# Moving transposes, filter loads and shared-expert products in a Hyena–SSD–MoE block, and removing the edge products of its long convolutions

## The chip, the cores and the metric

The kernel runs on one core of a Trainium2 chip. The metric is the device time of one execution in microseconds (us), the median of several runs. A core has five engines, each with its own instruction queue that runs strictly in order: TensorE (PE, matrix products), VectorE (DVE), ScalarE (ACT), GpSimd (POOL) and SyncE (SP, which only issues transfers here). Sixteen DMA engines move the data. POOL and ACT can issue transfers as well.

## The reference

One encoder block for 1024 tokens of width 1024, in float32:

```python
proj = u @ w_in + b_in                      # 1024 x 11328
k_spec = hyena_filters(seq, ...)            # implicit filters -> spectra
y_hy = hyena_mixer(p_hy, ..., k_spec, hy_bias) @ w_hy_branch
y_ssd = ssd_mixer(p_z, p_xbc, p_dt, ...) @ w_ssd_branch
g_hy, g_ssd = split(sigmoid(p_gate), 2)
mix = (g_hy * y_hy + g_ssd * y_ssd) @ w_out + b_out
h = layer_norm(alpha * h + mix)
h = layer_norm(alpha * h + moe(h))          # 64 experts, top 8, and a shared expert

def fft_long_conv(u, k_spec, bias):         # twice per channel
    uf = rfft(u, n=2 * seq)
    y = irfft(uf * k_spec, n=2 * seq)[:seq]
    return y + u * bias
```

The SSD mixer is a scan over 8 groups of 4 heads, in 8 chunks of 128 tokens and in both directions; its output is normalised by the root of a mean square for each group.

## The kernel before, in words

All wide products are made of three products of rounded parts (high by high, low by high, high by low), 128x512 each. Four stages follow one another.

**Front (to about 1325 us).** The input projection runs in slots. One slot is one block of 128 columns of `w_in`: eight k-steps of three products for two token halves (L174; in the trace a pair of halves is one entry x2, so a k-step has three entries). Everything else of this stage is hooked into slots by a table: `at(slot, when, f)` calls `f` at the beginning of a slot, ahead of k-step 0 to 7, or at its end. That table fixes the order on every queue. For each scan group g, `start[g]` is its first slot b. Its jobs are:

- `t1`, `t1x`, `t2`: transposes on PE of B and X into banks S, O and Y of PSUM (L291), each copied out by ACT (L292); `t2` ends with seven weighings of X on POOL (L313).
- `load_bc`, `side_e`: SP loads decay rows (`bcs`), DVE adds a mask (L379), ACT takes eight exponentials (L383).
- `states`, `states1`: PE products for the states (L329), a chain on DVE that adds them up (L331, L333, L334).
- `post1`: normalisation of the group that ends (DVE, short steps), then eight scalings on ACT (L431).
- `post2`: transposes of the result on PE (L438), copied out by ACT with a scale (L439), and stored by SP (L440).

The end of one group (`post1` and `post2` at slots b + 11 and b + 12) falls into the first slots of the next. Groups 1, 3 and 5 (`FILL4`) have one slot fewer, so that both `post2` fall into one slot. Between slots DVE and ACT run the short convolution of the block before (`conv`: L180, L183; `silu`: L592, L594), and POOL or DVE makes the low part of the weights (L163).

**Filters (1310 to 1530 us).** `hy_prep` loads `hS` and `w4` from POOL's queue. `hy_filters` loads decay tables `dec` (three buffers) and `brow` from SP's queue and the cosine tables from POOL's; PE makes filter blocks (L926, L927, and L929 for the bias row), DVE multiplies them by `dec` (L932), ACT and POOL or DVE split them (L73, L74), and PE multiplies by the cosines.

**Convolutions (1530 to 1770 us).** Eight items (four channel blocks, two filter orders). An item is folded (`fold`, L807 to L810), transposed (`analyse`, copied to `sdf` by ACT), multiplied by four frequency blocks kt (`forward`, L1054), combined with the filter spectrum on DVE (L1070 to L1090), and transformed back (L1107 to L1110). The even and odd samples lie in rows ty of `sdf`. One unpaired sample has a table of its own, `Fe`, and one extra matmul for each kt (L1056).

**Output projection and experts (1770 us to the end).** In `merge` the router's scores are 64-column products (`scores`, L78 to L80 into bank D). The shared expert is a generator, cut into chunks of three 128x512 products, that `route`, `early` and the end of the function advance. Then come 64 experts: SP loads weights `eraw`, ACT and DVE split them (`ehi` L1627, `elo` L1633), POOL gathers tokens (L1640), PE multiplies (L78 to L80).

Of the kernel before, what the change touches and what calls it, by code (L numbers as in the profile page):

```python
# [19 lines left out]
P = 128  # L20
# [4 lines left out]
KT = D // P  # L25
ALPHA = 2.0 ** 0.25


# [13 lines left out]
class Kern:  # L42
# [231 lines left out]
    def ssd_jobs(self, pool, pool2, g, tl):  # L274
# [149 lines left out]
        def post1():  # L424
            ss = S["ss"]
            TS(ss, ss, 1.0 / 256, 4e-5, ALU.mult, ALU.add)
            S["rs"] = pool.tile([P, 8], F32, name="rs", bufs=2)
            self.rsqrt(S["rs"], ss, pool, 8)
            for c in range(8):
                yz = S["zs"][:, c, :]  # L430
                nc.scalar.activation(yz, yz, AF.Copy, scale=S["rs"][:, c:c + 1])  # L431

        def post2(q):
            yo = S["zs"][:, :, q * P:(q + 1) * P]
            for h in range(2):
                pt = self.bank("SY"[h])
                for j in range(4):
# [4 lines left out]
        return dict(load_bc=load_bc, states1=states1, t1x=t1x, t1=t1, t2=t2, states=states, zs_tr=zs_tr, pe1=pe1, pe3=pe3, side_e=side_e, side_a=side_a, side_b=side_b,  # L442
                    side_c=side_c, post1=post1, post2=post2)

# [19 lines left out]
    def front(self):  # L464
# [4 lines left out]
        with ExitStack() as c2:  # L469
# [147 lines left out]
            for g in range(8):  # L617
                j = jobs[g]
                b = start[g]
                at(b, 4, j["t1"])  # L620
                at(b, 6, j["t1x"])
                at(b + 1, 3, j["t2"])
                at(b + 1, "end", j["states"])
                at(b + 2, 1, j["states1"])
                for q in range(2):
                    at(b + 2 + q, 3, lambda j=j, q=q: j["zs_tr"](q))
                at(b, "end", lambda j=j: j["load_bc"](0))
                for c in range(8):
                    at(b + 1 + c, "first", lambda j=j, c=c: j["side_e"](c))
                    at(b + 2 + c, 4, lambda j=j, c=c: j["pe1"](c))  # L630
                    at(b + 2 + c, "side", lambda j=j, c=c: j["side_b"](c))
                for c in range(8):
                    at(b + 1 + c, "side", lambda j=j, c=c: j["side_a"](c))
                    at(b + 3 + c, 5, lambda j=j, c=c: j["pe3"](c))
                    at(b + 4 + c, "begin", lambda j=j, c=c: j["side_c"](c))
                at(b + 11, "begin", j["post1"])
                for q in range(2):
                    def f(j=j, q=q, sl=b + 11 + q):
                        j["post2"](q)()
                    if q and g in FILL4:  # L640
                        at(b + 11, "side", f)
                    else:
                        at(b + 11 + q, 7 - 6 * q, f)
# [161 lines left out]
    def fold(self, u, sd):  # L805
        nc = self.nc
        rev = free(u[:, 512:513], [[-1, 512]])  # L807
        nc.vector.tensor_tensor(sd[:, 0], u[:, 512:1024], rev, ALU.add)
        nc.gpsimd.tensor_tensor(sd[:, 1], rev, u[:, 512:1024], ALU.subtract)
        nc.gpsimd.tensor_copy(sd[:, 1, 0:1], u[:, 0:1])  # L810

# [3 lines left out]
    def hy_prep(self):  # L815
# [14 lines left out]
        def s_load(m):  # L830
            nc.gpsimd.dma_start(S[m], self.S_d[:, m])
            load(m, slice(0, 256))
        s_load(0)
        nc.sync.dma_start(self.brow[0], a["hy_bias"][:, :, 0:256])
        yield
# [5 lines left out]
    def hyena(self):  # L841
        nc, a, tc = self.nc, self.a, self.tc
        self.K_d = self.scratch("K", (2, 4, 4, P, 1024))
        self.yhy_d = self.scratch("yhy", (D, L))
        if True:
            self.fp = tc.alloc_tile_pool(name="hyf", bufs=1, reuse_waits="tile")
            self.fs = tc.alloc_tile_pool(name="hys", bufs=1, reuse_waits="tile")
            self.sds, self.folds, self.Kt = {}, {}, {}
            self.sgn = self.fs.tile([P, 1], F32, name="sgn")
            nc.sync.dma_start(self.sgn, a["c_sgn"])  # L850
            for _ in self.flt:
                pass
            self.hy_convs()
# [19 lines left out]
    def analyse(self, k, j, tag):  # L873
        nc = self.nc
        if j == 0:
            self.sds[k] = (self.fs if k % 2 == 0 else self.fa).tile([P, 4, 2, 256], F32, name=f"sdf{k % 2}")
        sd = self.folds.pop((k, j))
        for q in range(2):
# [9 lines left out]
            if q == 0:  # L888
                nc.scalar.copy(d, ps)
            else:  # L890
                nc.scalar.copy(d[:, 0], ps[:, 0])
                nc.scalar.activation(d[:, 1], ps[:, 1], AF.Copy, scale=self.sgn)

    def hy_filters(self):
# [10 lines left out]
        def load_dec(i):  # L905
            if i < len(steps):
                b, m = steps[i]
                for h in range(2):
                    decs[i, h] = kp.tile([P, 4, 256], F32, name="dec", bufs=3)
                    nc.sync.dma_start(decs[i, h], a["c_dec"][m, b, :, h * 4:(h + 1) * 4])  # L910
                if m == 0:
                    br[b] = self.brow[b % 2]
                    if b > 0:
                        nc.sync.dma_start(br[b], a["hy_bias"][:, :, b * 256:(b + 1) * 256])
# [43 lines left out]
        with ExitStack() as cx:  # L958
# [3 lines left out]
            for i, (b, m) in enumerate(steps):  # L962
                if i == 2:
                    nc.sync.dma_start(Fm, a["c_F"])
                    Fe = self.Fe = self.fp.tile([P, 512], F32, name="Fe")
                    nc.gpsimd.memset(Fe, 0.0)
                    nc.scalar.copy(Fe[0:1], Fm[0:1, 2, 0])
                    self.sd_load(0)
# [38 lines left out]
    def hy_convs(self):  # L1007
# [7 lines left out]
        with ExitStack() as cx:  # L1015
# [5 lines left out]
            gts, zs, Z, inv, fw, sto = {}, {}, {}, {}, {}, []  # L1021
            Fm, Fe, sgn = self.Fm, self.Fe, self.sgn

# [16 lines left out]
            def forward(k, kt):  # L1040
# [6 lines left out]
                for par in range(2):  # L1047
                    for q in range(2):
                        ty = 2 * q + par
                        out = ps[:, par, q * 256:(q + 1) * 256]  # L1050
                        edge = par == 0 and q == 0
                        fy, fs = (ty, ksl) if ty < 3 else (1, slice((kt + 2) % 4 * P, ((kt + 2) % 4 + 1) * P))
                        for mt in range(2):
                            mm(out, Fm[:, fy, mt, fs], sd[:, ty, mt], start=mt == 0, stop=mt == 1 and not edge)  # L1054
                        if edge:
                            mm(out, Fe[:, ksl], sd[:, 2, 0], start=False, stop=True)  # L1056
                yc = pool.tile([P, 512], F32, name="yc", bufs=1)
# [171 lines left out]
    def merge(self):  # L1229
# [107 lines left out]
        with ExitStack() as cx:  # L1337
# [113 lines left out]

            def scores(t):
                for k, (xh, xl) in enumerate(lhs(t)):
                    self.mm3(psl[:, t * 64:(t + 1) * 64], xh, xl, rt[0][:, k], rt[1][:, k], k == 0, k == 7)

# [92 lines left out]
            for t in range(4, 8):  # L1548
# [4 lines left out]
                if t == 4:  # L1553
                    for _ in sh_down(0, hb):
                        pass
                    hb = sh_h(sg1)
                scores(t)
            wp.release()
            self.tabs()
            fill = rest(hb)  # L1560

# [758 lines left out]
def consts():  # L2320
# [23 lines left out]
    c["c_dec"] = np.ascontiguousarray(dec.transpose(0, 3, 2, 1, 4))  # L2344
    f = 4 * np.arange(512) + 1

# [11 lines left out]
    F[0][0] = 0.5  # L2358
    F[2][0] = w[0]
    c["c_F"] = np.ascontiguousarray(np.concatenate(F).astype(np.float32).reshape(3, 2, P, 512).transpose(2, 0, 1, 3))  # L2360
# [47 lines left out]
```

## Time and profile before

| | |
|---|---|
| median of 3 runs | 3216.88 us (3214.09 to 3218.8) |
| the profiled execution | 3221.08 us, its span 3219.3 us |
| PE, DVE, ACT, POOL busy | 94%, 69%, 48%, 28% |
| mean granted TensorE clock | 0.971 |

The span runs from the first to the last instruction. In the rows below a timeline entry is start, duration, engine, line, operation, tile written and tiles read; square brackets hold the idle time of the engine ahead of it and what ended that. A granted clock of 1.00 is 2.4 GHz and 0.50 is 1.2 GHz.

### The profile page before, as it was taken

What the parts mean: (1) busy time and instruction counts of PE and PEld (TensorE: products, weight loads), DVE (VectorE), ACT (ScalarE), POOL (GpSimd) and SP (SyncE); (2) the same over time, 40 slices, a digit from 0 to 9 for tenths busy, and PEclk for the clock granted to TensorE, in tenths of its full rate; (3) what the DMA queues carried; (4) which work ended last, traced back from release to release, by engine and by line L of the source; (5) the groups of instructions that cost most, each with busy time, mean ns of one, the idle gap of its engine ahead of it and who ended that gap; (6) DMA issues with size and microseconds to landing.
All of it is one profiled execution on the core that took longest, in us unless ns stands there. A gap on an engine that the chain in (4) does not pass through costs nothing.

```text
span 3219.3 us, 41385 instructions
## 1 busy us (share of the span) xinstructions
PE 3034.7 (94%) x14955; PEld 2457.2 (76%) x14955; DVE 2226.7 (69%) x3146; ACT 1544.8 (48%) x2573; POOL 901.6 (28%) x670
## 2 busy tenths in 40 slices
PE   8898999899989989899999999999899999999991
PEld 6786878787878878688888888887677777777771
DVE  6665666566666757565998244466688888888875
ACT  3544464546445544322222321242577777777772
POOL 2202020202011211343020041021254555555643
PEclk9999999999999999899999999998899999999996
DMA  4333432323242333654324444533899999999996
GB/s 140 74 88 75 99 86 82 92 86 82 81 102 71 109 82 98 173 184 173 125 92 144 138 163 132 161 105 128 261 322 324 327 331 323 316 312 317 321 300 173
DMA packets 343899, 546.54 MB, mean 170 GB/s; under 512 B 24617, under 2 KB 242509, under 8 KB 334989
## 3 DMA queue, kind: packets, MB, share of 16 engines
q1 hardware_dynamic: 316781, 450.54, 44.0%
q0 software_dynamic: 25760, 89.14, 11.3%
q10 hardware_dynamic: 1152, 4.19, 0.3%
q8 instruction: 119, 1.95, 0.2%
q14 instruction: 87, 0.71, 0.1%
HBM read 434.48 MB, written 109.32 MB: 169 GB/s over the span
## 4 chain that ended last, share of the span: by engine, by line
PE 79%; DVE 7%; ACT 5%; DMA 4%; issue 4%; POOL 1%; SPq 0%; ACTq 0%; DVEq 0%; POOLq 0%
PE bankA L174 24%; PE bankA L1312 8%; PE bankA L78 8%; PE bankA L79 7%; PE bankA L80 7%; PE bankI L1110 3%; PE bankA L1054 3%; PE bankA L1897 2%; PE bankB L1655 2%; PE bankA L1899 2%; PE bankY L373 2%; ACT bcs L383 1%; DMA bcs<-scr_at 1%; DMA scr_ace<-yo,sidx 1%; PE bankD L2116 1%
## 5 line engine op out<-in xcount | busy, mean ns | idle before, releaser
L174 PE MATMUL bankA<-xth,whi 128*128 128x512 f32 (+1 forms) x1424 | 474.3, 414 | 1.1 <-ACT whi L158 0.9
L174 PE MATMUL bankA<-xth,wlo 128*128 128x512 f32 (+1 forms) x1424 | 445.5, 394 | 1.5 <-POOL wlo L163 1.5
L174 PE MATMUL bankA<-xtl,whi 128*128 128x512 f32 (+1 forms) x1424 | 446.7, 395 | 0.0
L1633 DVE TENSOR_TENSOR elo<-eraw,ehi 128x2048 fp32r<-128x2048 f32 (+1 forms) x198 | 438.4, 2217 | 8.6 <-DMA scr_acc<-sr 8.6
L1627 ACT CAST ehi<-eraw 128x2048 fp32r<-128x2048 f32 (+1 forms) x198 | 356.8, 1858 | 5.8 <-DVE sr L1493 3.4
L174 PEld LDWEIGHTS bankA<-xth,wlo 128*128 128x128 f32 (+1 forms) x1424 | 268.7, 189 | 63.5 <-POOL wlo L163 1.9
L174 PEld LDWEIGHTS bankA<-xtl,whi 128*128 128x128 f32 (+1 forms) x1424 | 269.5, 189 | 60.7 <-DVE xtl L74 0.4
L174 PEld LDWEIGHTS bankA<-xth,whi 128*128 128x128 f32 (+1 forms) x1424 | 260.7, 191 | 54.8 <-issue 5.6
L1640 POOL DMA_INDIRECT xg<-scr_h,gidx x96 | 225.5, 2349 | 167.3 <-PE bankB L1655 128.2
L163 POOL TENSOR_TENSOR wlo<-wraw,whi 128x1024 fp32r<-128x1024 f32 (+1 forms) x35 | 83.4, 2383 | 638.8 <-ACT whi L158 623.3
L558 ACT ACTIVATE pin<-bankA,par 128x512 f32<-128x512 f32 x112 | 71.1, 687 | 331.6 <-PE bankA L174 331.4
L79 PE MATMUL bankA<-elo,xgh 128*128 128x512 f32 (+1 forms) x512 | 204.1, 399 | 9.0 <-DVE elo L1633 9.0
L78 PE MATMUL bankA<-ehi,xgh 128*128 128x512 f32 (+1 forms) x512 | 208.9, 408 | 0.3 <-ACT ehi L1627 0.3
L80 PE MATMUL bankA<-ehi,xgl 128*128 128x512 f32 (+1 forms) x512 | 203.2, 397 | 0.0
L383 ACT ACTIVATE bcs<-bcs,Acs 128x128 f32<-128x128 f32 x512 | 157.1, 396 | 50.3 <-DVE bcs L379 50.2
L1676 POOL DMA_INDIRECT scr_ace<-yo,sidx x48 | 124.5, 2593 | 177.8 <-ACT yo L1675 86.2
L183 DVE SCALAR_TENSOR_TENSOR accxs<-pin,parh,accxs 128x1024 f32<-128x1024 f32 x64 | 103.2, 1613 | 64.2 <-ACT accxs L180 61.4
L1676 POOL DMA_INDIRECT scr_acc<-yo,sidx x48 | 100.3, 2090 | 132.1 <-DVE yo L1936 65.5
L313 POOL TENSOR_TENSOR xw<-Xtok,wst 128x256 f32<-128x256 f32 x112 | 114.3, 1046 | 79.8 <-ACT Xtok L292 67.4
L1054 PE MATMUL bankA<-sdf,Fm 128*128 128x256 f32 x512 | 122.2, 382 | 2.2 <-DVE U L1071 2.2
L379 DVE TENSOR_TENSOR bcs<-bcs,negm 128x1024 f32<-128x1024 f32 x64 | 78.1, 1220 | 63.7 <-DMA bcs<-scr_at 63.7
L79 PEld LDWEIGHTS bankA<-elo,xgh 128*128 128x128 f32 (+1 forms) x512 | 95.4, 186 | 33.5 <-DVE elo L1633 12.2
(555 smaller groups left out, 6948.2 us busy)
## 6 DMA issues: line engine op xcount, KB each, us to landing
eraw<-in_exp_w_gate_dram SPq DMA_DIRECT2D x128, 512.0 KB
eraw<-in_exp_w_up_dram SPq DMA_DIRECT2D x128, 512.0 KB
eraw<-in_exp_w_down_dram SPq DMA_DIRECT2D x64, 1024.0 KB
wraw<-in_w_in_dram SPq DMA_DIRECT2D x88, 512.0 KB
bcs<-scr_at SPq DMA_DIRECT2D x128, 256.0 KB
scr_K<-kout SPq DMA_DIRECT2D x32, 512.0 KB
Kt<-scr_K SPq DMA_DIRECT2D x32, 512.0 KB
scr_gate<-accf SPq DMA_DIRECT2D x16, 512.0 KB
```

The source lines that it names most:

```text
L78: mm(out, sh, mh, start=first, stop=False)
L79: mm(out, sh, ml, start=False, stop=False)
L80: mm(out, sl, mh, start=False, stop=last)
L174: mm(ps[h], wt[:, k, :n], x[:, h * 512:(h + 1) * 512], start=(k == 0 and f == 1), stop=(k == KT - 1 and l == 1))
L313: GT(hq(xw), hq(S["X"][:, c, :]), hb(self.wst, c, d, 64), ALU.mult)
L383: nc.scalar.activation(E[:, d, h], E[:, d, h], AF.Exp, bias=self.A[:, c, j:j + 1])
L1054: mm(out, Fm[:, fy, mt, fs], sd[:, ty, mt], start=mt == 0, stop=mt == 1 and not edge)
L1312: mm(ps[h], w[:, k], al[h][q], start=(k == 0 and st == 1), stop=(k == 7 and en == 1))
L1627: nc.scalar.copy(whl[p][0][:, c], wraw[p][:, c])
L1633: nc.vector.tensor_tensor(lo[:, c], wraw[p][:, c], hi[:, c].bitcast(F32), ALU.subtract)
L1640: nc.gpsimd.indirect_dma_start(out=t[:n, :], out_offset=None, in_=self.h_d, in_offset=bass.IndirectOffsetOnAxis(ap=tabs[r][s][0], axis=0))
L1676: nc.gpsimd.indirect_dma_start(out=self.acc_d if b % 2 else self.ace_d, out_offset=bass.IndirectOffsetOnAxis(ap=tabs[r][s][1], axis=0), in ...
```

## The change

**Front.** `t1`, `t1x` and `t2` stood at k-step 4, k-step 6 and k-step 3 of the next slot for all groups. Now they stand at 7, 7 and (next slot) 3 for group 0, at k-steps 2, 3 and 4 of the first slot for groups 1, 3, 5 and 7, and where they were for groups 2, 4 and 6. The eight scalings of `post1` become `post1s`; for groups 0, 2, 4 and 6 they move from the beginning of slot b + 11 to its k-step 5.

**Filters.** The first `brow` and the first two `dec` loads go to POOL's queue.

**Convolutions.** The 512 frequencies are renumbered, even ones first in each half. With that order the unpaired sample has one constant factor with alternating sign by kt, so it can be merged into the row of the middle sample: `fold` scales it, `analyse` keeps a second version `sde` of row 0 for odd kt, and the 32 extra matmuls, `Fe`, its memset and its copy go. Added are 16 ACT copies (128x128), 16 POOL subtractions (1x128) and 16 DVE operations (128x1); 16 POOL copies (128x1) become multiplications.

**Experts.** The generator of the shared expert starts ahead of `scores(4)`, and `scores` of token blocks 4 to 7 takes one chunk at each odd k, 16 in all.

```diff
+        def post1s():
             for c in range(8):
                 yz = S["zs"][:, c, :]
                 nc.scalar.activation(yz, yz, AF.Copy, scale=S["rs"][:, c:c + 1])
...
-                at(b, 4, j["t1"])
-                at(b, 6, j["t1x"])
-                at(b + 1, 3, j["t2"])
+                h = (7, 7, 11) if g == 0 else (4, 6, 11) if g - 1 in FILL4 else (2, 3, 4)
+                for n, w in zip(("t1", "t1x", "t2"), h):
+                    at(b + w // 8, w % 8, j[n])
...
                 at(b + 11, "begin", j["post1"])
+                at(b + 11, "begin" if g in FILL4 or g == 7 else 5, j["post1s"])
...
-        nc.gpsimd.tensor_copy(sd[:, 1, 0:1], u[:, 0:1])
+        nc.gpsimd.tensor_scalar(sd[:, 1, 0:1], u[:, 0:1], 2 * R2, None, ALU.mult)
+        nc.vector.scalar_tensor_tensor(sd[:, 0, 0:1], u[:, 0:1], R2, sd[:, 0, 0:1], ALU.mult, ALU.add)
...
+        nc.gpsimd.dma_start(self.brow[0], a["hy_bias"][:, :, 0:256])
         s_load(0)
-        nc.sync.dma_start(self.brow[0], a["hy_bias"][:, :, 0:256])
...
             if q == 0:
                 nc.scalar.copy(d, ps)
+                nc.scalar.copy(self.sde[k][:, j * P:(j + 1) * P], ps[:, 0, 0])
             else:
                 nc.scalar.copy(d[:, 0], ps[:, 0])
+                r0, e0 = self.sds[k][0:1, :, 0, j * P:(j + 1) * P], self.sde[k][0:1, j * P:(j + 1) * P]
+                nc.gpsimd.tensor_tensor(e0, r0[:, 0], r0[:, 2], ALU.subtract)
...
-                    nc.sync.dma_start(decs[i, h], a["c_dec"][m, b, :, h * 4:(h + 1) * 4])
+                    (nc.sync if i else nc.gpsimd).dma_start(decs[i, h], a["c_dec"][m, b, :, h * 4:(h + 1) * 4])
...
-                        edge = par == 0 and q == 0
+                        rows = [sd[:, ty, mt] for mt in range(2)]
+                        if ty == 0 and kt % 2:
+                            rows[0] = self.sde[k]
...
-                            mm(out, Fm[:, fy, mt, fs], sd[:, ty, mt], start=mt == 0, stop=mt == 1 and not edge)
-                        if edge:
-                            mm(out, Fe[:, ksl], sd[:, 2, 0], start=False, stop=True)
+                            mm(out, Fm[:, fy, mt, fs], rows[mt], start=mt == 0, stop=mt == 1)
...
-            def scores(t):
+            def scores(t, fill=None):
                 for k, (xh, xl) in enumerate(lhs(t)):
+                    if fill and k % 2:
+                        next(fill, None)
                     self.mm3(psl[:, t * 64:(t + 1) * 64], xh, xl, rt[0][:, k], rt[1][:, k], k == 0, k == 7)
...
-                    hb = sh_h(sg1)
-                scores(t)
+                    fill = rest(sh_h(sg1))
+                scores(t, fill)
             wp.release()
             self.tabs()
-            fill = rest(hb)
...
-    f = 4 * np.arange(512) + 1
+    f = 4 * np.concatenate([np.arange(o, o + 256, 2) for o in (0, 1, 256, 257)]) + 1
...
-    F[2][0] = w[0]
+    F[2][0] = np.sign(w[0]) / 4
```

ACT's queue where group 1 begins, before (`Btok` and `Xtok` are the copies behind `t1`, `t1x` and `t2`, `zs` the result of group 0):

```order
L431 ACTIVATE zs<-zs,rs 128x256 x8
L292 COPY Btok<-bankS 128x512
L292 COPY Btok<-bankO 128x512
L292 COPY Xtok<-bankS 128x4x128
L439 ACTIVATE zs<-bankS,par 128x4x128
L439 ACTIVATE zs<-bankY,par 128x4x128
L558 ACTIVATE pin<-bankA,par 128x512 x2
L158 ACTIVATE whi<-wraw 128x1024
L180 ACTIVATE accC<-pin,parh 128x1024
L383 ACTIVATE bcs<-bcs,Acs 128x128 x8
L439 ACTIVATE zs<-bankS,par 128x4x128
L439 ACTIVATE zs<-bankY,par 128x4x128
```

The same place of ACT's queue in the changed kernel, whose line numbers are larger by up to 3:

```order
L293 COPY Btok<-bankS 128x512
L293 COPY Btok<-bankO 128x512
L293 COPY Xtok<-bankS 128x4x128
L293 COPY Xtok<-bankO 128x4x128
L293 COPY Xtok<-bankS 128x4x128
L293 COPY Xtok<-bankY 128x4x128
L434 ACTIVATE zs<-zs,rs 128x256 x8
L442 ACTIVATE zs<-bankS,par 128x4x128
L442 ACTIVATE zs<-bankY,par 128x4x128
L561 ACTIVATE pin<-bankA,par 128x512 x2
L159 ACTIVATE whi<-wraw 128x1024
L181 ACTIVATE accC<-pin,parh 128x1024
```

The six copies now stand together ahead of the eight scalings; three of them stood behind the exponentials (L383) and the last two L439.

POOL's queue where the filters begin, before (`w4l`, `w4h` and `hS` are the filter network's operands):

```order
L831 DMA hS_10082<-scr_S 128x1024
L828 DMA w4h_10079<-scr_w4h 64x2x256 x2
L828 DMA w4l_10080<-scr_w4l 64x2x256
L948 DMA cose<-in_c_cose_dram 128x1024 x2
L831 DMA hS_10078<-scr_S 128x1024
L828 DMA w4h_10075<-scr_w4h 64x2x256 x2
L828 DMA w4l_10076<-scr_w4l 64x2x256
L951 DMA coso<-in_c_coso_dram 128x2048 x2
L74 TENSOR_TENSOR kl<-kr,kh 128x512
```

The same place of POOL's queue in the changed kernel:

```order
L838 DMA brow_10081<-in_hy_bias_dram 1x2x256
L836 DMA hS_10090<-scr_S 128x1024
L833 DMA w4h_10087<-scr_w4h 64x2x256 x2
L833 DMA w4l_10088<-scr_w4l 64x2x256
L920 DMA dec<-in_c_dec_dram 128x1024 x2
L958 DMA cose<-in_c_cose_dram 128x1024 x2
L836 DMA hS_10086<-scr_S 128x1024
L833 DMA w4h_10083<-scr_w4h 64x2x256 x2
L833 DMA w4l_10084<-scr_w4l 64x2x256
L961 DMA coso<-in_c_coso_dram 128x2048 x2
L75 TENSOR_TENSOR kl<-kr,kh 128x512
```

The two `dec` loads stand ahead of the cosine tables, the second set of `hS` and `w4`, and POOL's first split.

PE's queue at the scores of token block 6, in the changed kernel (`rth`, `rtl` are the router's weights in bank D; `wh`, `wl` and `ld` belong to the shared expert):

```order
L1452 MATMUL bankB<-ident,sr 128x128 x8
L79 MATMUL bankD<-rth,bh 128x64
L80 MATMUL bankD<-rtl,bh 128x64
L81 MATMUL bankD<-rth,bl 128x64
L79 MATMUL bankA<-wh,ld 128x512
L80 MATMUL bankA<-wl,ld 128x512
L81 MATMUL bankA<-wh,ld 128x512
L79 MATMUL bankD<-rth,bh 128x64
L80 MATMUL bankD<-rtl,bh 128x64
L81 MATMUL bankD<-rth,bl 128x64
L79 MATMUL bankD<-rth,bh 128x64
L80 MATMUL bankD<-rtl,bh 128x64
```

Before, the 24 products of a token block into bank D stood there without the 128x512 products between them; those stood behind the last product of `early`.

## Rows read from the trace of the kernel before

**Rows 1.** Busy time of each engine over the span, from the page

```profile
PE 3034.7 (94%) x14955; PEld 2457.2 (76%) x14955; DVE 2226.7 (69%) x3146; ACT 1544.8 (48%) x2573; POOL 901.6 (28%) x670
```

**Rows 2.** Stretches: PE, PEld, DVE, ACT, POOL busy (instructions), granted clock, DMA share, GB/s

```profile
1540.00:1760.00 220.00, 220.00 (x1072) 195.06 (x1072) 209.49 (x270) 51.00 (x139) 28.08 (x20) 1.00 0.34 109
...
2165.00:2190.00 25.00, 24.26 (x123) 22.83 (x123) 7.24 (x11) 5.59 (x9) 4.72 (x2) 0.60 0.18 70
...
2250.00:2260.00 10.00, 10.00 (x53) 8.34 (x50) 4.72 (x19) 0.77 (x2) 2.97 (x3) 1.00 0.50 171
...
2270.00:2280.00 10.00, 2.78 (x7) 2.20 (x8) 4.73 (x8) 4.49 (x5) 0.00 (x0) 0.50 0.70 239
```

**Rows 3.** Timeline of PE where group 1 begins

```profile
276.86 1.12 PE L291 MATMUL bankS<-ident,accxs 128*128 128x128 f32 x4 [9.09 <-ACT zs L439]
...
280.33 1.05 PE L174 MATMUL bankA<-xth,wlo 128*128 128x512 f32 x2
...
285.09 0.63 PE L174 MATMUL bankA<-xtl,whi 128*128 128x512 f32 x2
```

**Rows 4.** Timeline of ACT at the same place

```profile
254.18 3.32 ACT L431 ACTIVATE zs<-zs,rs 128x256 f32<-128x256 f32 x8 [3.09 <-DVE rs L462]
...
273.77 2.46 ACT L383 ACTIVATE bcs<-bcs,Acs 128x128 f32<-128x128 f32 x8 [8.24 <-DVE bcs L379]
276.13 0.67 ACT L439 ACTIVATE zs<-bankS,par 128x512 f32<-128x512 f32 x1
```

**Rows 5.** Timeline of DVE at the same place, and last where group 7 begins

```profile
272.51 1.23 DVE L379 TENSOR_TENSOR bcs<-bcs,negm 128x1024 f32<-128x1024 f32 x1 [16.09 <-DMA bcs<-scr_at]
273.66 5.31 DVE L183 SCALAR_TENSOR_TENSOR accC<-pin,parh,accC 128x1024 f32<-128x1024 f32 x4
...
280.44 1.67 DVE L594 SCALAR_TENSOR_TENSOR accC<-pin,accC 128x1024 f32<-128x1024 f32 x1 [0.46 <-ACT pin L592]
288.05 0.42 DVE L331 COPY st<-bankO 128x256 f32<-128x256 f32 x1 [5.94 <-PE bankO L329]
...
1211.03 0.42 DVE L331 COPY st<-bankO 128x256 f32<-128x256 f32 x1 [4.58 <-PE bankO L329]
```

**Rows 6.** Timeline of PE in the first slot of group 0

```profile
100.09 1.09 PE L291 MATMUL bankS<-ident,accB 128*128 128x128 f32 x4 [7.75 <-DVE accB L594]
```

**Rows 7.** The chain that ended last where the filters begin

```profile
1323.40 8.11 DMA scr_gate<-accf
1331.58 10.83 DMA dec<-in_c_dec_dram
```

**Rows 8.** Timelines of ACT, DVE and PE at the same place

```profile
1329.18 3.31 ACT L431 ACTIVATE zs<-zs,rs 128x256 f32<-128x256 f32 x8 [3.10 <-DVE rs L462]
1335.02 1.23 ACT L73 ACTIVATE kh<-kr 128x512 fp32r<-128x512 f32 x2 [2.54 <-DVE kr L932]
...
1342.53 1.29 DVE L932 TENSOR_TENSOR kr<-bankA,dec 128x512 f32<-128x512 f32 x2 [1.75 <-DMA dec<-in_c_dec_dram]
...
1348.27 1.12 PE L438 MATMUL bankS<-ident,zs 128*128 128x128 f32 x4 [7.81 <-ACT zs L439]
```

**Rows 9.** The extra products of line L1056: shortest, median, longest in ns; first, last start

```profile
L1056 PE MATMUL bankA<-sdf,Fe x64: 379/379/634, 1515.9 to 1743.4; 128*128 128x256 f32 x64
```

**Rows 10.** Timeline of DVE inside the convolutions

```profile
1616.70 0.15 DVE L1146 COPY zc<-y 128x1 f32<-128x1 f32 x1
...
1619.41 2.29 DVE L1077 TENSOR_TENSOR M<-U,Kt 128x1024 f32<-128x1024 f32 x1
...
1629.68 1.22 DVE L1077 TENSOR_TENSOR M<-U,Kt 128x1024 f32<-128x1024 f32 x1
```

**Rows 11.** Timeline of POOL at the same place

```profile
1618.26 2.36 POOL L1150 TENSOR_TENSOR zc<-zc,gt 128x1024 f32<-128x1024 f32 x1 [25.73 <-DVE zc L1149]
```

**Rows 12.** Timelines of SP and PE where the experts begin

```profile
2264.77 0.34 SPq L1616 DMA_DIRECT2D eraw<-in_exp_w_gate_dram  x1
...
2277.22 0.80 PE L79 MATMUL bankA<-elo,xgh 128*128 128x512 f32 x1 [9.02 <-DVE elo L1633]
```

More of the change, by code (lines that the diff above doesn't have):

```diff
@@ L26 @@
 ALPHA = 2.0 ** 0.25
+R2 = 2.0 ** 0.5
 def bcast(ap, dims):
@@ L442, in ssd_jobs @@
         return dict(load_bc=load_bc, states1=states1, t1x=t1x, t1=t1, t2=t2, states=states, zs_tr=zs_tr, pe1=pe1, pe3=pe3, side_e=side_e, side_a=side_a, side_b=side_b,
-                    side_c=side_c, post1=post1, post2=post2)
+                    side_c=side_c, post1=post1, post1s=post1s, post2=post2)
     def rsqrt(self, out, v, pool, n):
@@ L847, in hyena @@
             self.fs = tc.alloc_tile_pool(name="hys", bufs=1, reuse_waits="tile")
-            self.sds, self.folds, self.Kt = {}, {}, {}
+            self.sds, self.sde, self.folds, self.Kt = {}, {}, {}, {}
             self.sgn = self.fs.tile([P, 1], F32, name="sgn")
@@ L875, in analyse @@
         if j == 0:
-            self.sds[k] = (self.fs if k % 2 == 0 else self.fa).tile([P, 4, 2, 256], F32, name=f"sdf{k % 2}")
+            fp = self.fs if k % 2 == 0 else self.fa
+            self.sds[k] = fp.tile([P, 4, 2, 256], F32, name=f"sdf{k % 2}")
+            self.sde[k] = fp.tile([P, 256], F32, name=f"sde{k % 2}")
         sd = self.folds.pop((k, j))
@@ L964, in hy_filters @@
                     nc.sync.dma_start(Fm, a["c_F"])
-                    Fe = self.Fe = self.fp.tile([P, 512], F32, name="Fe")
-                    nc.gpsimd.memset(Fe, 0.0)
-                    nc.scalar.copy(Fe[0:1], Fm[0:1, 2, 0])
                     self.sd_load(0)
@@ L1021, in hy_convs @@
             gts, zs, Z, inv, fw, sto = {}, {}, {}, {}, {}, []
-            Fm, Fe, sgn = self.Fm, self.Fe, self.sgn
+            Fm, sgn = self.Fm, self.sgn
             def load_g(k, j):
```

## The prediction

> **What bounds the kernel now.** I read the page first: PE is busy 94% of the span, DVE 69% [rows 1], so the time is PE's work plus the holes in it, and a hole counts only where PE has no other work in its queue. The table of stretches then shows what kind of stage each edit touches. In the convolutions PE has no hole at all, but DVE is busy 209.49 of 220 us beside it; at the scores PE is busy 24.26 of 25 us, at a granted clock of 0.60; where the experts begin it works 2.78 of 10 us [rows 2]. Last I went to PE's timeline at each place that the diff names, and from each hole back over the queues: ACT, DVE, then the transfer.
>
> **Front, groups 1, 3, 5 and 7.** PE stands 9.09 us before the second batch of `t2` because bank S is held by a copy L439 on ACT [rows 3]. That copy starts at 276.13, right behind the exponentials, which waited 8.24 us for DVE's L379 [rows 4], which waited 16.09 us for `bcs` [rows 5]. So a transpose whose inputs are long there waits for a load it has nothing to do with. Behind the hole PE runs at the lower level, 1.2 GHz: an entry of two matmuls takes 1.05 us at 280.33 and 0.63 at 285.09 [rows 3]. DVE feels it at L331, which waits 5.94 us for PE until 288.05; DVE had ended L594 at 280.44 + 1.67 = 282.11 [rows 5].
>
> With `t2` at k-step 4 PE passes here and comes to the state products early. The `bcs` chain stays: L379 lands where it did, L183 and L594 follow, and L331 is now ready at 282.1. PE will still wait, for L439 to give up bank S at the first state products and then for L331 to give up bank O; the hole is shorter and sits later. What DVE waited at L331 is won: 5.94 us at the first of the four places, 4.58 at the last [rows 5], mean 5.26, times four 21.0. The seven weighings leave the side of L594, which then can take the 1.23 of L379 (same width) in place of 1.67: four times 0.44 is 1.8. Against that PE's stretch at half rate does not vanish; it slides behind L331, beside the DVE chain. Five entries at 1.05 for 0.63 are 2.1 us; I charge a third, 0.7 for each place, 2.8. Sum 20.0.
>
> The eight scalings, 3.32 us on ACT, move behind the six copies. ACT idled 3.09 us ahead of them [rows 4], so the copies fill that hole and the scalings end about where they did; queued behind them are L439, and behind that on SP the store and the `bcs` load. If the cover fails, each place loses up to 3.32, 13 in all, and A comes to 7.
>
> **Front, group 0.** PE waits 7.75 us for the silu of B (L594) [rows 6]. `t1` moves three k-steps back, each six matmuls. A wide matmul at full rate costs 0.23 us: the stretch 2250 to 2260 has 53 in 10 us, ten of them small [rows 2]. So 3 x 6 x 0.23 = 4.1 us of work goes into the hole: 4.
>
> **Filters.** The chain is a gate store (8.11 us), then the second `dec` that waits for its memory (10.83), then L932 at 1342.53 [rows 7]. On POOL's queue the second `dec` waits for that same store, and queued behind it are the cosine tables, the second `hS` and `w4` loads and POOL's first split. Those loads ran beside the store and `dec` before; held back, they leave both more room. What can be won is the 1.75 us by which L932 waits for the second `dec`, and at the start the distance from the end of L431 (1332.49) to the first split (1335.02), 2.5 us, since ACT is the next in line there [rows 8]. That is 4.2; I take 4. The other end: the held loads come late by half of one landing in this crowd, 5 us lost.
>
> The Trainium skill ("DMA: Bandwidth & Descriptors", Issuing engine by pattern) says that simple loads belong on SP and that its hardware queue is generally faster than GpSimd's. By its first-byte figures, 0.6 against 1 us, an estimate from the page would take 0.4 us off each of two loads, the sum 36 in place of 37; landings of 8 to 11 us [rows 7] hide such a difference, and no row here separates it.
>
> **Convolutions.** The extra products are 64 records [rows 9]. With 1072 records in 220 us a record costs 0.205 us [rows 2], so PE loses 13.1 us of work, and it is the engine without a hole. But DVE has only 220 - 209.5 = 10.5 us free, and gets 8 more small operations in this stage, by the nearest row 0.15 each [rows 10], 1.2 in all. So the stage can shrink by 9.3 at the very best, and only if no wait of DVE on PE remains. DVE's order is fixed and its cycle runs nearly full already; once PE is faster, PE waits for the combined spectra (U) instead. And DVE's operations stretch beside POOL: L1077 takes 2.29 us while POOL's L1150 runs, 1.22 otherwise [rows 10, 11]. More POOL instructions, 16 subtractions, now fall into this stage; at worst each spoils a fifth of that 1.07, about 3 us. Bounds -3 and +9; I take +2, nearer to DVE's end, since DVE's row is the fuller after the change.
>
> The Trainium skill ("GPSIMD Engine Reference", 1. Specifications) says that POOL's SBUF interfaces are shared with VectorE and contend when DVE has two SBUF inputs. The trace agrees (2.29 against 1.22); by the rule alone, with no PE gain let through, this part would be -3 and the sum 32.
>
> **Scores and the way to the experts.** At a mean of 0.60 between the levels 0.5 and 1.0, 80% of the 25 us run at 1.2 GHz, though PE is nearly always busy; only narrow products and transposes stand there [rows 2]. Sixteen chunks of three wide products, 48 x 0.23 = 11.0 us, now lie between them. If the clock holds, the old work takes 25 - 10 = 15 us, with the chunks 26; the splits that half rate hid open a hole of about 1 us (my choice) at each of three transposes: the scores end some 4 us later. At the end 11.0 us of chunks are gone. SP issues the first expert weights when the last chunk is through (2264.77), and PE has its first operands 12.45 us later, at 2277.22, after a wait of 9.02 [rows 12]. That wait stays; the whole start moves by 11 - 4 = 7. If the clock stays low at the scores the chunks cost 22 there, and the part is -11 at worst.
>
> **Sum.** 20 + 4 + 4 + 2 + 7 = 37 us off the profiled execution: 3221.08 - 37 = 3184.1. That execution is 4.2 above the median of the runs, 3216.88, so I forecast 3179.9, say 3180 us.
>
> **Rivals.**
> 1. The edge products pay in full. For it: PE without a hole over 220 us [rows 2]. Against it: DVE's 209.5. With 9 in place of 2, and the upper ends elsewhere (group starts 22.8), 3180 - 7 - 3 = 3170.
> 2. The wait only changes its name. At the group starts PE meets L439 and L331 with the scalings in the way, A is 7 to 13, and the scores' clock stays at 0.60 so that D gives nothing: 3180 + 10 + 7 = 3197. For it: half rate follows even holes that I leave in place. Against it: ACT's idle 3.09 covers the move.
> 3. Slower than before: the merged row comes late. `sde` for odd kt is made by ACT's copy and then by POOL's subtraction, in POOL's queue with L1150 and the folds; PE's first product of kt = 1 waits for it, and DVE's cycle behind PE. A cycle of DVE is 10.27 us where POOL works (1619.41 to 1629.68) [rows 10]. If half of it, 5.1 us, is lost in each of 8 items, that is 41, and the time 3180 + 2 + 41 = 3223. It decides from 5.2 us an item. Against it: POOL idles 25.73 us ahead of L1150 [rows 11], room for a subtraction in each item.
> 4. The convolutions turn out bound by DVE entirely (-3) and POOL's queue, held by the second `dec`, costs 5 in place of winning 4: 3180 + 5 + 9 = 3194.
>
> **Chances.** Forecast 0.50 (own range 3174 to 3187), rival 1 0.15, rival 2 0.17, rival 3 0.06, rival 4 0.12. The range 3167 to 3199 leaves out rival 3 and the far ends. About 0.2%, 6.4 us, is what a measurement here tells from no change: faster than 3210.4 are all but rival 3 and the worst ends of 2 and 4 together: 0.89 faster, 0.05 within, 0.06 slower.
>
> **What would show it.** Right: no wait of 7 to 9 us at the transposes of `t2`; L331 4 to 6 us closer to L594 at four places; the wait on accB for group 0 near 3.6; L932's second `dec` without its 1.75; granted clock near 1 at the scores and SP's first `eraw` some 7 us nearer to them. In the convolutions PE should show holes that end on DVE, with the stage nearly as long as before. Wrong: a stage of convolutions shorter by over 6 us (DVE was not the bound), or waits on `sde`; PE idle at the second `w4` or cosine loads; the same total hole at the group starts, with L331 no earlier.

## The result and the profile after

The changed kernel takes 3195.13 us (median of 4 runs, 3189.02 to 3196.41) against 3216.95 before (3214.09 to 3218.8): ratio 0.9929, 95% interval 0.9912 to 0.9946, so it is 21.8 us faster. The profiled execution took 3195.61 us, span 3193.8, clock 0.974. The forecast was 3180, from 37 us of gain; 22 came.

The gain lies in the front alone. Where group 1 begins, the timeline of PE in the changed kernel (lines are larger by 1 to 8) shows two short holes at the state products where 9.09 us stood at the transposes [rows 3]:

```profile
273.55 0.67 PE L330 MATMUL bankS<-xw,Btok 128*128 128x256 f32 x2 [2.48 <-ACT zs L442]
...
279.82 1.22 PE L330 MATMUL bankS<-xw,Btok 128*128 128x256 f32 x2 [3.21 <-DVE st L335]
```

ACT at the same place: the copies come first and the scalings follow without a gap, where ACT idled 3.09 us ahead of the scalings before [rows 4]:

```profile
247.75 0.58 ACT L293 COPY Btok<-bankS 128x512 f32<-128x512 f32 x1
...
252.99 3.31 ACT L434 ACTIVATE zs<-zs,rs 128x256 f32<-128x256 f32 x8
...
272.74 0.67 ACT L442 ACTIVATE zs<-bankS,par 128x512 f32<-128x512 f32 x1
```

DVE at the same place: the long wait for `bcs` stays, and the first state copy follows L597 with no wait, where it waited 5.94 us [rows 5]:

```profile
269.13 1.23 DVE L380 TENSOR_TENSOR bcs<-bcs,negm 128x1024 f32<-128x1024 f32 x1 [15.96 <-DMA bcs<-scr_at]
...
277.22 1.23 DVE L597 SCALAR_TENSOR_TENSOR accC<-pin,accC 128x1024 f32<-128x1024 f32 x1 [0.16 <-ACT pin L595]
278.36 0.42 DVE L332 COPY st<-bankO 128x256 f32<-128x256 f32 x1
```

PE in group 0, where 7.75 us stood [rows 6]; 1.10 us is a new wait, for the copy out of bank S:

```profile
99.77 0.63 PE L292 MATMUL bankS<-ident,accB 128*128 128x128 f32 x4 [3.65 <-DVE accB L597]
...
101.94 1.11 PE L292 MATMUL bankS<-ident,accxs 128*128 128x128 f32 x4 [1.10 <-ACT Btok L293]
```

The other three parts gave nothing or cost. PE's waits (line waited for, us in total, times, longest) from 1290 to 1325, where the filters begin, and from 1484 to 1746, the convolutions:

```profile
PE bankA L936 <- DMA w4h<-scr_w4h: 7.7, 1, 7.7
PE bankS L441 <- ACT zs L442: 6.0, 1, 6.0
```

```profile
PE bankA L1063 <- DVE U L1078: 13.9, 10, 2.6
```

At the scores the clock now holds (the stretch's columns are those of rows 2, where 0.60 stood):

```profile
2135.00:2163.00 28.00, 26.33 (x172) 23.31 (x171) 9.84 (x15) 5.54 (x10) 4.78 (x2) 1.00 0.23 91
```

But in the routing behind them DVE stands 5.16 us for ACT's part of a shared-expert activation (L1878). The router's own steps, the expert numbers (`eid`) and `r_parts`, are queued behind it:

```profile
2188.92 0.24 DVE L2279 TENSOR_SCALAR r_pm<-iota,r_rk 64x64 bf16<-64x64 f32 x1
2194.32 0.42 DVE L1878 TENSOR_TENSOR ld<-ld,bankA 128x256 f32<-128x256 f32 x1 [5.16 <-ACT ld L1877]
2194.66 0.20 DVE L2286 CAST eid<-bankA 1x64 int32<-1x64 f32 x1
2194.79 0.40 DVE L2287 CAST r_parts<-r_b 128x512 bf16<-128x512 f32 x1
```

At `eid` 31.3 us have passed since the last score, against 27.4 in the kernel with the hooks alone, so this wait accounts for 3.9 us of a routing that is 7.8 us longer. The rest grows behind it. DVE's first copy of an early table (`tb`) is 5.3 us late, and it waits 4.46 us for PE where the hooks-alone kernel (second line) waits 0.81:

```profile
2213.36 0.17 DVE L2132 COPY tb<-bankD 128x12 f32<-128x12 f32 x1 [4.46 <-PE bankD L2124]
```

```profile
2201.59 0.17 DVE L2127 COPY tb<-bankD 128x12 f32<-128x12 f32 x1 [0.81 <-PE bankD L2119]
```

This table sets the kernels of the study side by side; the experiments that they belong to follow below, and the last three compute something else. Each entry is the difference of two starts in PE's timeline: front, from the span's start to the last projection product; conv, from the first forward product to the last inverse one; scores, from the first score to the last; routing, from there to the last early-table product; start, from there to the first product with `elo`.

| kernel | front | conv | scores | routing | start |
|---|---|---|---|---|---|
| before | 1321.6 | 260.0 | 78.6 | 62.1 | 27.4 |
| changed | 1293.6 | 261.5 | 83.2 | 70.0 | 17.2 |
| hooks alone | 1294.7 | 259.8 | 77.0 | 62.2 | 27.5 |
| filter loads alone | 1319.3 | 259.8 | 76.7 | 61.0 | 27.4 |
| convolutions alone | 1320.3 | 260.3 | 76.7 | 61.0 | 26.6 |
| chunks alone (16) | 1320.7 | 259.8 | 83.2 | 69.1 | 17.3 |
| hooks, 12 chunks | 1289.5 | 259.8 | 80.1 | 63.9 | 27.3 |
| hooks, 4 chunks | 1293.6 | 259.8 | 80.5 | 68.3 | 22.3 |
| hooks without moved scalings | 1326.1 | 259.8 | 78.7 | 62.2 | 26.4 |
| hooks, new convolutions, small operations on ScalarE | 1291.3 | 260.8 | 77.1 | 62.3 | 25.2 |
| before, VectorE lighter | 1320.5 | 257.4 | 77.8 | 63.9 | 27.2 |
| changed, VectorE lighter | 1289.7 | 246.4 | 83.2 | 71.2 | 17.7 |
| changed, without GpSimd's subtractions | 1291.4 | 257.5 | 83.2 | 71.1 | 18.0 |

Between kernels with the same code the front varies by 2 to 5 us and the scores by 2; conv varies by 0.2 with the old code and by 1.2 with the new (260.3 and 261.5). The filters, from the end of the front to the first forward product, take 190.5 to 193.3 in every one.

### The profile page after: what moved, and what is told of

Same layout as the page of the kernel before. It is cut to its first block, busy times and chain, and to the rows that moved or that the text cites. A ratio compares the mean times of both kernels' runs of the same rounds, so it can differ in the third digit from the quotient of the medians.

```text
span 3193.8 us, 41307 instructions
## 1 busy us (share of the span) xinstructions
PE 3018.1 (94%) x14890; PEld 2439.2 (76%) x14891; DVE 2231.3 (70%) x3162; ACT 1543.8 (48%) x2588; POOL 905.2 (28%) x688
## 3 DMA queue, kind: packets, MB, share of 16 engines
q0 software_dynamic: 26080, 90.19, 11.4%
## 4 chain that ended last, share of the span: by engine, by line
PE 75%; DVE 11%; DMA 5%; issue 4%; ACT 3%; POOL 1%; SPq 0%; ACTq 0%; DVEq 0%; POOLq 0%
PE bankA L175 26%; PE bankA L1319 8%; PE bankA L79 8%; PE bankA L81 7%; PE bankA L80 7%; PE bankA L1905 2%; PE bankB L1663 2%; PE bankA L1907 2%; PE bankY L374 2%; PE bankI L1117 1%; DMA bcs<-scr_at 1%; DVE M L1084 1%; DVE M L1086 1%; PE bankA L1063 1%; PE bankS L362 1%
## 5 line engine op out<-in xcount | busy, mean ns | idle before, releaser
L561 ACT ACTIVATE pin<-bankA,par 128x512 f32<-128x512 f32 x112 | 71.1, 687 | 333.2 <-PE bankA L175 333.0
L380 DVE TENSOR_TENSOR bcs<-bcs,negm 128x1024 f32<-128x1024 f32 x64 | 78.0, 1219 | 59.3 <-DMA bcs<-scr_at 59.3
L1063 PE MATMUL bankA<-sdf,Fm 128*128 128x256 f32 x480 | 111.4, 385 | 3.5 <-DVE U L1078 3.5
```

The lines of the kernel that those rows point to most:

```text
L1063: mm(out, Fm[:, fy, mt, fs], rows[mt], start=mt == 0, stop=mt == 1)
```

## The experiments

**The hooks alone.** Edit to the kernel before:

```diff
-                at(b, 4, j["t1"])
-                at(b, 6, j["t1x"])
-                at(b + 1, 3, j["t2"])
+                h = (7, 7, 11) if g == 0 else (4, 6, 11) if g - 1 in FILL4 else (2, 3, 4)
+                for n, w in zip(("t1", "t1x", "t2"), h):
+                    at(b + w // 8, w % 8, j[n])
...
+                at(b + 11, "begin" if g in FILL4 or g == 7 else 5, j["post1s"])
```

> The kernel before with the scan hooks alone. Theory (the parts add up, each with the shift that the two traces show at the end of its stage): 28 us faster, nearly all of it at the four group starts (6.4, 7.2, 6.5, 5.5) and 3 to 4 at group 0; ratio 0.991. Rival (the forecast's sum, where half rate behind the shorter hole eats part): 24 us or less, ratio 0.9925. The half rate behind the first state products should be seen either way.

Measured: 3189.76 us against 3216.63, ratio 0.9913 (0.9896 to 0.9929), 26.9 us faster. That is all of the gain. By the medians it is more than the whole change gives, though the two intervals overlap.

**The filter loads alone.**

```diff
-                    nc.sync.dma_start(decs[i, h], a["c_dec"][m, b, :, h * 4:(h + 1) * 4])
+                    (nc.sync if i else nc.gpsimd).dma_start(decs[i, h], a["c_dec"][m, b, :, h * 4:(h + 1) * 4])
```

> The kernel before with the first brow and dec loads on GpSimd's queue alone. Theory: 2 to 4 us faster by the end of the filters, ratio 0.999, no verdict by time. Rival: the second dec, waiting for the gate store, holds the queue and the filters end as late as before or later (0 to +5 us).

Measured: 3218.38 against 3216.63, ratio 1.0005 (0.9995 to 1.0014): nothing. The number is within the rival's range, but neither hole that was named decides. POOL's timeline in this kernel shows another: `brow` is the first load of its queue and waits 3.25 us until a projection product (L174) ends, and all other loads stand behind it:

```profile
1319.76 0.72 POOL L833 DMA_DIRECT2D brow<-in_hy_bias_dram  x1 [3.25 <-PE bankA L174]
...
1321.06 1.26 POOL L828 DMA_DIRECT2D w4h<-scr_w4h  x2
```

In the kernel with the convolutions alone, whose front ended 1.0 us later, POOL issued `w4h` 2.8 us sooner:

```profile
1318.24 1.28 POOL L830 DMA_DIRECT2D w4h<-scr_w4h  x2
```

PE of the kernel with the filter loads waits 7.48 us at its first filter product, where the kernel with the convolutions alone waits 3.1 there and 3.8 at the bias row. The row names ACT; in the changed kernel the same wait is put down to `w4h`:

```profile
1328.22 0.77 PE L926 MATMUL bankA<-w4h,hS 128*128 128x512 f32 x1 [7.48 <-ACT zs L431]
```

**The convolutions alone.** The edit is the whole convolution part of the change; this is its core:

```diff
-                            mm(out, Fm[:, fy, mt, fs], sd[:, ty, mt], start=mt == 0, stop=mt == 1 and not edge)
-                        if edge:
-                            mm(out, Fe[:, ksl], sd[:, 2, 0], start=False, stop=True)
+                            mm(out, Fm[:, fy, mt, fs], rows[mt], start=mt == 0, stop=mt == 1)
```

> The kernel before with the change of the convolutions alone. Theory (VectorE binds this stage once the edge products are gone): the stage is 1 to 2 us longer, with some 14 us of new waits of TensorE for the combined spectra; ratio 1.000. Rival (the stage is bound by TensorE, and the loss seen comes from what stands ahead of it): 5 to 13 us shorter, ratio 0.997.

Measured: 3215.96 against 3216.63, ratio 0.9998 (0.9989 to 1.0008); the stage 260.3 against 259.8, with 13.9 us of waits for U. The products went and their time came back as waits.

**The same stage with VectorE lighter, before and after.** From both kernels one operation for each frequency block is taken. They then compute something else, so their whole times (3260.09 and 3216.33 us, one run each) say nothing here and only the convolutions are read.

```diff
-                TT(U[:, 1], M[1][:, 0], M[1][:, 1], ALU.subtract)
```

> The kernel before without one VectorE operation in each frequency block of the convolutions (the subtraction that ends the complex product is left out, 32 x 0.69 = 22 us of VectorE). Theory (before, TensorE bound this stage, VectorE close behind): from the first product of the convolutions to their last inverse product 255 to 260 us in place of 260. Rival (VectorE bound it before, too): 240 to 245.

> The changed kernel without the same VectorE operation. Theory (VectorE binds once the edge products are gone, so with VectorE lighter their 13 us show): 244 to 249 us for the convolutions in place of 261.5, some 10 us below the cut kernel before; TensorE's waits for the combined spectra mostly gone. Rival (the edge products were not worth 13 us, or the merged row's way over ScalarE and GpSimd holds TensorE): 255 us or more, within 4 of the cut kernel before.

Measured: 257.4 and 246.4 us for the convolutions. The stretch of the convolutions, columns as in rows 2, of the hooks-alone kernel (old convolutions), the convolutions alone, the cut kernel before and the cut kernel after:

```profile
1485.53:1745.33 259.80, 256.35 (x1249) 226.68 (x1249) 236.56 (x305) 62.71 (x162) 28.09 (x20) 1.00 0.41 132
```

```profile
1511.03:1771.31 260.28, 246.21 (x1184) 215.24 (x1185) 241.44 (x313) 63.91 (x177) 36.87 (x35) 0.99 0.41 132
```

```profile
1513.42:1770.82 257.40, 256.30 (x1249) 226.73 (x1250) 217.69 (x273) 62.86 (x162) 28.11 (x20) 1.00 0.41 134
```

```profile
1480.19:1726.62 246.43, 244.23 (x1184) 215.50 (x1185) 221.38 (x281) 65.06 (x177) 37.56 (x35) 0.99 0.43 139
```

Read the busy times of PE and DVE against the stretch. The old stage is bound by PE (256 of 260), and 19 us less of DVE shorten it by 2.4. Without the edge products PE has 246 and the stage does not move; take DVE's 20 us off as well and 11.0 of PE's time show. Both engines had to be relieved. PE's waits for U fall from 13.9 to 2.2 us in the changed kernel.

**Without GpSimd's subtractions.** One line less in the changed kernel:

```diff
-                nc.gpsimd.tensor_tensor(e0, r0[:, 0], r0[:, 2], ALU.subtract)
```

> The changed kernel without GpSimd's 16 subtractions for the second version of the middle row (row 0 for odd frequency blocks is then not right). Theory (VectorE binds the convolutions, and its additions and products stretch beside GpSimd): 1 to 3 us off the 261.5 of the stage, and the mean of the two products and the subtraction on VectorE back to that of the kernel before. Rival (TensorE waits for the merged row itself): its waits for the combined spectra stay and the stage shrinks by more than 5.

Measured: the stage takes 257.5 us (the whole 3188.44, one run). That is 4.0 less than in the changed kernel and 2.8 less than in the kernel with the convolutions alone, which has the same code there, so at the upper end of the theory's range. DVE's means of two of its operations, changed kernel first (busy us, mean ns):

```profile
L1086 DVE TENSOR_TENSOR M<-U,Kt 128x1024 f32<-128x1024 f32 x32 | 44.2, 1380 | 0.0
...
L1088 DVE TENSOR_TENSOR U<-M 128x512 f32<-128x512 f32 x32 | 23.8, 744 | 0.0
```

```profile
L1085 DVE TENSOR_TENSOR M<-U,Kt 128x1024 f32<-128x1024 f32 x32 | 42.5, 1329 | 0.0
...
L1087 DVE TENSOR_TENSOR U<-M 128x512 f32<-128x512 f32 x32 | 22.8, 712 | 0.0
```

DVE executes the same operations and is busy 237.8 in place of 241.6 us; the 3.8 us are what 16 operations on one partition cost it. The product is back at its mean in the kernel before (1330 ns), the subtraction only half of the way (684). PE's waits for U stay at 10.7 us without the subtractions, and no wait of PE is put down to the merged row.

**Small operations moved to ScalarE**, with the hooks and the new convolutions (by its median the best of the measured versions):

```diff
+            nc.scalar.activation(sd[:, 1, 0:1], u[:, 0:1], AF.Copy, scale=2 * R2)
+            nc.scalar.activation(sd[:, 0, 0:1], u[:, 0:1], AF.Identity, bias=sd[:, 0, 0:1], scale=R2)
...
-                nc.vector.tensor_copy(y[:, 0:1], y0)
+                nc.scalar.copy(y[:, 0:1], y0)
```

> The scan hooks and the change of the convolutions, with the small operations of the fold and the copy of one column moved from VectorE and GpSimd to ScalarE inside the convolutions (16 VectorE operations of 0.15 us and 8 of GpSimd go). Theory (VectorE binds, and ScalarE has room): the stage takes 257 to 259 us in place of 261.5, and the whole is 1 to 3 us faster than the hooks alone, ratio 0.990. Rival (ScalarE's queue, in order, now waits for the fold and holds the copies that TensorE's products need): 262 us or more, ratio 0.992.

Measured: 3185.46 us, ratio 0.9901 (0.9881 to 0.9921), not told apart from the hooks alone by its interval. The stage takes 260.8, between the two theories, so the convolutions are no part of a gain. DVE's time fell by 1.1 us only: four of its products now take 3.56 us, where the longest of the changed kernel takes 2.52.

**The chunks alone.**

```diff
+                    if fill and k % 2:
+                        next(fill, None)
```

> The kernel before with the shared expert's chunks among the scores alone, 16 of them. Theory (16 is not a whole number of token blocks of 12 chunks, so other chunks fall among the routing steps, and VectorE, in order, waits there for the shared expert's activation): scores end 4 to 5 us later, the last product of the early tables some 12 us later, the first expert 2 us later; ratio 1.000 to 1.001. Rival (the forecast): the routing takes as long as before and the first expert starts 7 us sooner, ratio 0.998.

Measured: 3220.48 against 3216.63, ratio 1.0017 (1.0007 to 1.0027): slower by some 4 us. Scores 83.2, routing 69.1 and start 17.3, against about 77, 62 and 27 without chunks.

**12 chunks, and 4,** with the hooks: `if fill and k in (1, 3, 5)` and `if fill and k == 1`.

> The kernel before with the scan hooks, and with 12 chunks (one whole token block of the shared expert: k = 1, 3, 5) among the scores instead of 16. Theory (the place in the token block at which the routing meets the generator sets its length): from the last score to the last product of the early tables 61 to 62 us as before, not 69 to 70; scores 4 to 5 us longer than the 77 of the kernel with the hooks alone; from there to the first expert 7 to 8 shorter; in all 2 to 3 us faster than the hooks alone, ratio to before 0.990. Rival (any chunk ahead of the routing makes it longer, since the generator's work on ScalarE and VectorE is then late): the routing takes 67 us or more, ratio 0.993.

> The kernel before with the scan hooks, and with 4 chunks of the shared expert among the scores (k = 1 of each token block). 4 and 16 chunks leave the generator at the same place in a token block of 12. Theory (that place decides): the routing, from the last score to the last product of the early tables, takes 68 to 70 us as with 16, against 62 without chunks and 63.9 with 12; scores about 2 us longer than 77. Rival (the routing grows with the number of chunks taken ahead of it): 62 to 64 us.

Measured: routing 63.9 with 12 chunks and 68.3 with 4 (3194.94 us in all, one run). Fewer chunks made the routing longer, so it is not their number: 4 and 16 leave the generator at the same place in its block of 12, and that place lengthens the routing. DVE's wait of 5.1 to 5.3 us behind `r_pm` is there with 4 and with 16 chunks, and with 12 and with none it is not. With 12 the total did not get better (3190.43, ratio 0.9919, 0.9904 to 0.9934), against the expectation: the start took 27.3 as without chunks. PE and POOL there:

```profile
2228.85 0.91 PE L1659 MATMUL bankB<-ident,xg 128*128 128x128 f32 x3 [8.30 <-DMA xg<-scr_h,gidx]
```

```profile
2221.85 1.06 POOL L1644 DMA_INDIRECT xg<-scr_h,gidx  x1 [24.57 <-DVE wt L2094]
```

Six chunks are left there. PE has two of them ahead of the transposes of the first gathered tokens and four behind. The gather takes 7.0 us from issue to use, with little left to hide it, and the shared expert's last store, for which the first `elo` waits, comes after the last chunk.

In the hooks-alone kernel DVE passes the place of the 5.16 us wait without one:

```profile
2183.70 0.24 DVE L2274 TENSOR_SCALAR r_pm<-iota,r_rk 64x64 bf16<-64x64 f32 x1
2183.86 0.41 DVE L74 TENSOR_TENSOR ld<-bankC,ld 128x256 fp32r<-128x256 f32 x1
2184.22 0.21 DVE L2281 CAST eid<-bankA 1x64 int32<-1x64 f32 x1
```

**The moved transposes without the moved scalings.**

```diff
-                at(b + 11, "begin" if g in FILL4 or g == 7 else 5, j["post1s"])
+                at(b + 11, "begin", j["post1s"])
```

> The kernel before with the moved transposes, but with the eight scalings at the beginning of the slot as before. Theory (the moved scalings are needed as cover: ahead of the copies they would hold them until the normalisation is done): the copies of the transposes wait some 6 us, TensorE waits for banks at the transposes, and each of the groups 1, 3, 5 and 7 wins 2 to 4 us less than with both moves; first state products of group 1 later than 272. Rival (the place of the scalings does not matter, the copies are early enough anyway): within 1 us of the kernel with both moves at each group.

Measured: 3221.52 us (one run), the front 1326.1: the whole gain is gone, and some 5 us more. PE and ACT where group 1 begins; the scalings stand ahead of the copies and wait for DVE's normalisation:

```profile
253.24 1.12 PE L291 MATMUL bankS<-ident,accxs 128*128 128x128 f32 x4 [5.50 <-ACT Btok L292]
```

```profile
249.42 3.30 ACT L433 ACTIVATE zs<-zs,rs 128x256 f32<-128x256 f32 x8 [3.08 <-DVE rs L464]
252.63 0.56 ACT L292 COPY Btok<-bankS 128x512 f32<-128x512 f32 x1
```

The hole at the second transposes is 5.26 to 6.27 us at the four group starts, and PE runs at 1.2 GHz behind it (granted clock 0.50 from 253.3 to 257.5). What follows on ACT and SP moves back: `bcs` reaches DVE at 275.61, 3.1 us later than before, although this kernel was 4.7 us ahead until then. Against the kernels with both moves 8 us are lost at each place, twice the upper end of what was expected (2 to 4). The scalings moved without the transposes were not run.

## Why the prediction was right or wrong

**The time fell within the range (3167 to 3199), and the sum was wrong in every part.** From the table: the front gives 28.5 us (mean of the seven kernels with both moves, 1292.0, against 1320.5 for the kernels with the old hooks), the filters 0, the convolutions -0.5 to -1.7, the experts' part -4.0 (scores, routing and start together: 170.0 in the two kernels with 16 chunks that compute the block, 166.0 in the six without chunks). That is 22.8 to 24.0 against 21.8 measured. In part the range was kept by luck: the front's 4.5 us too little set off some of the experts' 11 too much. The time lies outside the narrower range of the forecast alone (3174 to 3187), and nearer to the numbers of rivals 4 and 2 (3194, 3197), though not by their mechanisms.

**Front: the mechanism was right, the size too small.** 20 + 4 were forecast. L332 follows L597 with no wait and the wait for accB is 3.65 as said (3.6). PE's holes are nearly those that were named: L442 for bank S, and then the state chain, on L335 just behind the L331 (now L332) of the text. The shift at the four group starts was 6.4, 7.2, 6.5 and 5.5 us, the sum 25.6 in place of 20; group 0 gave 2.9. What DVE waited at L331 was 5.94, 4.62, 5.76 and 4.58 us, 20.9 in all, so the 21.0 held. Two terms were mis-sized. The charge for half rate, 2.8, was hardly paid: PE does run at half rate behind the second hole, but from the first state copy to DVE's next wait for PE the four places take 10.9 to 11.6 us, against 11.3 to 11.4 before. And `bcs` does not land quite where it did: counted from the same slot, L380 stands 0.2 to 1.8 us sooner, and L597 2.6 us in all.

The bound for the scalings, 13, was for scalings that end late behind the copies. At group 1 they do end 2.0 us later, counted from the same slot, and `bcs` is not late for it. What the sum had no price for is the transposes without the moved scalings, 31 to 34 us of front.

**Filters: 4 forecast, 0 measured.** The step "what can be won is the 1.75 us by which L932 waits for the second `dec`" rested on one execution: in the kernel with the convolutions alone, whose loads are the old ones, that wait is not there. The other, 2.5 us at the first split, overlooked that the split waits for L929, and L929 for the first `w4h`, which now stands behind `brow`. The rule on POOL's queue was not tested by this, since an order in the queue and not its speed decided; the `dec` loads on POOL's queue without `brow` were not run.

**Convolutions: 2 forecast, -0.5 to -1.7 measured.** The reading was right: DVE binds as soon as PE is faster, and PE waits for U. The end of the range that was chosen was still too high. The extra products were worth 10 to 12 us of PE's busy time (13.1 forecast), of which nothing came through. DVE's 8 small operations cost the 1.2 us forecast (236.6 before, 237.8 without GpSimd's subtractions). The price of POOL's subtractions was put at up to 3 us; it is 2.8 to 4.0. The contention that the Trainium skill states ("GPSIMD Engine Reference", 1. Specifications) is what the experiment shows, 744 against 712 ns.

**Experts: +7 forecast, -4 measured. This step failed.** The terms that were written are nearly right: the scores took 4.6 to 6.5 us more (4 forecast, and the clock holds at 1.00), the start 9.3 to 10.2 less (11 forecast). What the sum left out is the stage between them. It took for granted that `route` and `early`, drawing as many chunks as before, take as long; but they draw other chunks, and DVE, in order, meets the activation of a token block in the middle of the router's chain. The routing is 7 to 8 us longer, the whole of the forecast gain; half of that is lost by `eid`, and the steps behind it were not followed one by one.

One row was misread, without harm to the sum. The loads at 2264.77 [rows 12] are not those of the first expert: in the kernel before SP issues five loads of weights from 2227.67 on. DVE's first `elo` is held, by its row, by the shared expert's last store (`scr_acc`), which ACT issues at 2265.49:

```profile
2227.67 0.36 SPq L1616 DMA_DIRECT2D eraw<-in_exp_w_gate_dram  x1
...
2265.49 0.33 ACTq L1495 DMA_DIRECT2D scr_acc<-sr  x1
...
2275.27 4.91 DVE L1633 TENSOR_TENSOR elo<-eraw,ehi 128x512 fp32r<-128x512 f32 x8 [8.61 <-DMA scr_acc<-sr]
```

That store and the loads at 2264.77 both come right behind the last chunk, so the wait moves with the chunks either way.

**Rivals.** The first, edge products paying in full, is refuted by the convolutions alone, and the pair of cut kernels shows why. The second did not come: the wait did not only change its name, and the clock held. The third did not come: PE waits for U and not for `sde`. The fourth, convolutions bound by DVE and nothing from the filters, is nearest for two parts, but for the filters its mechanism, the second `dec`, was not the one.

## What to carry to other kernels

When work is pulled out of a side stream to fill a hole, count not only how much of it goes but where the stream then stands when the next stage draws on it: four chunks more or less shifted an activation into an in-order queue that a critical chain needed. An edit that takes work off the busiest engine is worth at most what the second busiest leaves. Here two busy times, 256 and 237 of 260 us, gave the warning, but by them alone some of the 10 us could still have come; that none did was seen only by taking work off the second engine. And where two edits move work past each other in one queue, test them apart: the transposes without the scalings gave nothing.

## What the runs showed of the hardware

A hole of the same length at the same kind of place is followed by the full clock or by the half. Where groups 1 and 3 end, PE of the changed kernel waits for the same copy ahead of the first transposes of `post2`:

```profile
417.86 0.66 PE L441 MATMUL bankS<-ident,zs 128*128 128x128 f32 x4 [2.42 <-ACT Xtok L293]
...
418.98 1.20 PE L175 MATMUL bankA<-xth,whi 128*128 128x512 f32 x2
```

```profile
720.22 0.66 PE L441 MATMUL bankS<-ident,zs 128*128 128x128 f32 x4 [2.41 <-ACT Xtok L293]
...
721.12 0.71 PE L175 MATMUL bankA<-xth,whi 128*128 128x512 f32 x2
```

The 3.1 us from there, columns as in rows 2:

```profile
417.86:420.96 3.10, 3.10 (x13) 2.65 (x14) 2.26 (x2) 2.65 (x4) 3.10 (x4) 0.61 0.02 5
720.17:723.27 3.10, 3.05 (x21) 2.67 (x22) 2.35 (x3) 2.74 (x5) 3.10 (x4) 1.00 0.00 0
```

Two wide products take 1.20 us behind one hole and 0.71 behind the other. It is not the place alone: in the kernel with the hooks and 12 chunks, whose front is the same code, group 1 stays at the full clock (1.00 from 414.9 to 418.0). Its lead over the kernel before is 12.5 us on both sides of this place, while that of the changed kernel falls from 9.6 to 8.8. So such a place costs 0.8 us or nothing, and the front has three of them. This is one source of the spread between runs of one code; that it is the only one is not shown. A term of 1 or 2 us read from one execution, like the 1.75 of `dec`, is within that spread.
